# Seven products of layer 1 in another order, one weight sum by VectorE; the last chunk block by block, the last norm by VectorE alone

## The chip, the core and the metric

The kernel runs on one core of a Trainium2 chip, as one launch. The metric is the device time in microseconds, median of several runs. The engines of a core are TensorE (PE in the profile; its weight loads PEld), VectorE (DVE), ScalarE (ACT), GpSimd (POOL) and SyncE (SP), which here issues DMAs. Each engine works through its own queue in order.

## The reference, cut to what matters

Two layers of a backbone over 512 latent tokens of width 2048 (and 256 context tokens, which only layer 0 uses). The change is in layer 1:

```python
xm = x_lat * (1.0 + sc_l) + sh_l                       # 512 x 2048
u, v, z = jnp.split(xm @ w_in, 3, axis=-1)             # w_in 2048 x 6144
v = layer_norm(v, ln_g, ln_b)
s = jnp.einsum('hts,bnshc->bnthc', w_sp, vh) + b_sp    # per 128 tokens and head
y = u * s * jax.nn.silu(z)
x = layer_norm(alpha * x_lat + g_l * (y @ w_out), post_ln_g, post_ln_b)   # w_out 2048 x 2048
```

All of it is float32. A product is made of three matmuls: each operand is split into a high part (rounded to the type fp32r) and a low part, the rest; high x high, high x low and low x high are added up.

## The kernel before, in words

**Layer 1's input product** is done in six jobs of 1024 columns, n = 0 to 5: two for v (`first` = 2, those with a `place`), then z, u, z, u. Each job is a 2 by 2 block product done with seven half-size products in place of eight. A product p has four steps, j = 0 to 3; one step is 12 matmuls of 128x512 (L1226 to L1228). The list `self.steps` in the class `Quarters` sets the order of TensorE's work. In it products 1 and 2 of jobs 0 and 1 stand first (as a block, while the context of layer 1's input is still being made), then for each job the groups of L1149.

A product's weight operand is a quarter of the weights (`wq`, 512 KB per step) or a sum of quarters. How each operand comes about:
- A raw load by SP (`raw`, tile `qr`) goes to one of four raw buffers (`crw0` and three `wraw`), in turn.
- In jobs 0 and 1 sums are made by DMAs that POOL issues and that add into what lies in the tile (`add`, L1163). Product 7 adds two quarters in a raw tile. A pair tile per j (`t1`) is loaded and added to for product 5, added to again for 6 (after 5's operand is split), and again for 4 (after 6's).
- In jobs 2 to 5 VectorE makes the sums of products 1 and 7 (L1203 and L1197); the pair tile still gets its additions for 6 and 4 from POOL.

`split` (L104 to L106) makes each operand's high part on ScalarE (L105) and its low part on VectorE (L106). They go to seven unit buffers in turn. `prep` runs two steps ahead of TensorE's step (QAHEAD), the loads three more (LAHEAD).

**The evacuation** of a finished product (`run`, L1237 to L1270) adds and subtracts the products' results and hands blocks to a `sink`. `combine` (before L1117) makes the activations' sums for products 5, 7, 6 and 3 of all jobs and splits them.

**The output product** (`out_phase` L953, `form_b` L186) goes in four chunks of 512 columns. For each of 16 row blocks of the weights (a part; `weights`, `ahead`), it does 3 matmuls (L202 to L204) for each of four blocks of 128 tokens. In the last chunk this holds for the first 4 parts only. The other 12 (HOLD) are kept, and each token block takes them in one go. When a token block is done, VectorE evacuates it (L964, L965, L967), and the final norm follows (`norm1`, L1408): three quarters of the row by VectorE (L1418, L1419), one by POOL, ScalarE and POOL (L1413 to L1416). POOL also takes the power for the standard deviation (L246). Each quarter is stored by its own DMA.

Of the kernel before, what the change touches and what calls it, by code (L numbers as in the profile page):

```python
# [10 lines left out]
F32 = mybir.dt.float32  # L11
# [57 lines left out]
def tile_backbone(ctx: ExitStack, tc: tile.TileContext, io: dict, out: bass.AP):  # L69
# [74 lines left out]
    AHEAD, HOLD = 2, 12  # L144
# [12 lines left out]
    def ahead(p):  # L157
        while len(parts) < min(p + AHEAD + 1, 2 * upto[0]):
# [6 lines left out]
            held = q - (2 * len(stream) - 8)  # L165
            if held >= 0:
                hi = big.tile([P, 512], F32R, tag=f"xh{2 * held}", name=nm("wh"))
                lo = big.tile([P, 512], F32R, tag=f"xh{2 * held + 1}", name=nm("wl"))
            else:
                hi, lo = halves()  # L170
# [917 lines left out]
    def combine():  # L1088
# [21 lines left out]
        for g in range(4):  # L1110
            after(ve.tensor_tensor, comb[3, g], comb[6, g], comb[3, g], ALU.subtract)
            yield PACE
            after(comb_split, 3, g, (big, f"xh{2 * g}"), (big, f"xh{2 * g + 1}"))
            yield PACE
        free = [f"mr{n}" for n in (4, 5, 6, 7, 0, 1, 2)] + ["mx"]
        for g in range(4):
            after(comb_split, 6, g, (la, free[2 * g]), (la, free[2 * g + 1]))  # L1117
            yield PACE
# [20 lines left out]
    class Quarters:  # L1139
# [5 lines left out]
        def __init__(self, jobs, first):  # L1145
            self.jobs, self.first = jobs, first
            self.steps = [(n, p_, j) for p_ in (1, 2) for n in range(first) for j in range(4)]
            for n in range(len(jobs)):
                for group in ((5, 7), (3,), (6,), (4,)) if n < first else ((1, 5, 7), (2, 3), (6,), (4,)):  # L1149
                    self.steps += [(n, p_, j) for j in range(4) for p_ in group]  # L1150
            self.rtags, self.utags = ["crw0"] + ["wraw"] * 3, ["araw"] * 3 + ["whl"] * 4
            self.n_r = self.n_u = 0
            self.loaded, self.made, self.t1 = [], [], {}
# [10 lines left out]

        def load(self, n, p_, j):
            first = n < self.first
            if p_ == 5 and first:
                self.t1[j] = pair_tile(j)
                dma.dma_start(self.t1[j], io["wq"][self.jobs[n][0], j, 1])
                self.add(self.t1[j], n, j, 0)  # L1170
                rs = []
            elif p_ == 7 and first:
                rs = [self.raw(n, j, 1)]
                self.add(rs[0], n, j, 3)
            elif p_ == 1 and not first:
                rs = [self.raw(n, j, 1), self.raw(n, j, 0)]
            else:
                rs = [self.raw(n, j, {1: 0, 7: 3, 2: 2, 3: 3}[p_])] if p_ in (1, 7, 2, 3) else []
            self.loaded.append(rs)
# [6 lines left out]
        def prep(self, upto):  # L1186
            while len(self.made) < min(upto, len(self.steps)):
# [5 lines left out]
                if p_ in (5, 6, 4):  # L1193
                    x_ = self.t1[j]
                elif p_ == 7 and n >= self.first:
                    x_ = self.b12[j]
                    ve.tensor_tensor(x_, x_, rs[0], ALU.add)  # L1197
                else:
                    x_ = rs[-1]
                    if p_ == 1 and n >= self.first:  # L1200
                        self.b12 = getattr(self, "b12", {})
                        self.b12[j], self.t1[j] = rs[0], pair_tile(j)
                        ve.tensor_tensor(self.t1[j], x_, rs[0], ALU.add)  # L1203
# [3 lines left out]
                if p_ in (5, 6):  # L1207
                    self.add(self.t1[j], n, j, 3 if p_ == 5 else 2)

        def run(self):  # L1210
            bank, w_, q57 = {}, {}, {}
            for i, (n, p_, j) in enumerate(self.steps):
# [17 lines left out]
                if p_ == 4 and j > 1:  # L1230
                    sink(*c22[j - 2])
                if j < 3:
                    continue
                neg = lambda x_: lambda o: ve.scalar_tensor_tensor(o, x_[0], -1.0, x_[1], ALU.mult, ALU.subtract)
# [7 lines left out]
                elif p_ == 5:  # L1242
                    q57[n] = [la.tile([P, 512], F32, tag="t2", name=nm("qc"), bufs=4) for _ in range(2)]
                    for t in range(2):
                        sc.copy(q57[n][t], pts[t])
                elif p_ == 7:
                    for t in range(2):
# [289 lines left out]
```

## Time and profile before

| | |
|---|---|
| median of 3 runs | 1743.78 us (1741.64 to 1746.02) |
| the profiled run | 1744.94 us |
| its span | 1743.1 us |
| mean granted clock of TensorE | 0.994 |
| PE busy | 98% of the span |
| DVE, ACT, POOL busy | 68%, 39%, 5% |
| DMA | 366.62 MB, mean 210 GB/s |

Durations in the text are from the profiled run; its span is 1.84 us shorter than its time. Times within the span count from its start. PE's busy share is an average: where TensorE waits is seen in windows, not here.

### The profile page before, as it was taken

To read this page: it belongs to the slowest core of one execution; us is meant where nothing else is said; L and a number is where in the kernel's file an instruction comes from. 1 tells how busy PE (TensorE), PEld (TensorE's weight loads), DVE (VectorE), ACT (ScalarE), POOL (GpSimd) and SP (SyncE) were. 2 spreads that over 40 slices of the span, in tenths; PEclk is the share of its full clock that TensorE was granted. 3 is DMA by queue.
4 is the path that set the end of the run, shared out by engine and by line. 5 is a ranking of instruction groups with operands and counts; after the bars stand their busy time and mean duration, and the time that the engine had idled before them with its cause. 6 is when DMAs were issued, how large, how long until landed. Compare 5 with 4: busy or idle time off the path is not lost.

```text
span 1743.1 us, 22763 instructions
## 1 busy us (share of the span) xinstructions
PE 1709.7 (98%) x8260; PEld 1398.9 (80%) x8260; DVE 1193.1 (68%) x2113; ACT 686.3 (39%) x1190; POOL 94.4 (5%) x129
## 2 busy tenths in 40 slices
PE   9999999999999999999999999989999999999995
PEld 5777788888888888888888888868887888788884
DVE  5875486556798886867644478857775767665557
ACT  4222232323544454445432257533544354432221
POOL 0000000000000000000000001220100100000004
PEclk9999999999999999999999999999999999999998
DMA  9986277879678575663483568996757576665442
GB/s 344 374 318 226 85 245 239 285 261 324 222 266 282 197 247 169 219 199 110 131 256 121 145 232 269 238 237 161 238 140 225 138 231 139 197 167 162 131 140 101
DMA packets 143295, 366.62 MB, mean 210 GB/s; under 512 B 13522, under 2 KB 29866, under 8 KB 142670
## 3 DMA queue, kind: packets, MB, share of 16 engines
q1 hardware_dynamic: 126574, 322.69, 54.6%
q0 software_dynamic: 9216, 33.56, 10.7%
q10 hardware_dynamic: 7392, 8.91, 1.4%
q8 instruction: 65, 1.06, 0.2%
q14 instruction: 48, 0.39, 0.1%
HBM read 340.42 MB, written 24.69 MB: 209 GB/s over the span
## 4 chain that ended last, share of the span: by engine, by line
PE 89%; DMA 5%; DVE 4%; issue 1%; ACT 0%; POOL 0%; POOLq 0%; ACTq 0%; DVEq 0%; SPq 0%
PE ps L202 10%; PE ps L204 10%; PE ps L203 10%; PE ps L1227 7%; PE ps L1228 7%; PE ps L1226 7%; PE ps L187 6%; PE ps L186 6%; PE ps L191 6%; PE ps L455 2%; PE ps L457 2%; PE ps L671 2%; PE ps L456 2%; DMA qr<-in_wq_dram 2%; DMA pair<-in_wq_dram 1%; PE ps L374 1%
## 5 line engine op out<-in xcount | busy, mean ns | idle before, releaser
L105 ACT CAST wh<-wr 128x512 fp32r<-128x512 f32 x344 | 211.7, 621 | 467.8 <-PE ps L204 284.2
L106 DVE TENSOR_TENSOR wh<-wr,wh 128x512 fp32r<-128x512 f32 x336 | 230.0, 687 | 208.1 <-ACT wh L105 206.3
L204 PE MATMUL ps<-wh,yl 128*128 128x512 f32 x512 | 199.5, 390 | 0.0
L202 PE MATMUL ps<-wh,yh 128*128 128x512 f32 x512 | 193.6, 391 | 0.0
L203 PE MATMUL ps<-wh,yh 128*128 128x512 f32 x480 | 187.2, 390 | 0.0
L186 PE MATMUL ps<-xh,wh 128*128 128x512 f32 x448 | 175.5, 392 | 0.0
L187 PE MATMUL ps<-xl,wh 128*128 128x512 f32 x448 | 174.8, 390 | 0.0
L191 PE MATMUL ps<-xh,wh 128*128 128x512 f32 x448 | 174.6, 390 | 0.0
L272 DVE SCALAR_TENSOR_TENSOR adw<-adw,crow 128x1024 f32<-128x1024 f32 x128 | 155.8, 1217 | 3.3 <-DMA adw<-in_adat_dram 3.2
L1227 PE MATMUL ps<-wh,ch 128*128 128x512 f32 x384 | 150.6, 395 | 4.0 <-DVE wh L106 4.0
L1228 PE MATMUL ps<-wh,ch 128*128 128x512 f32 x384 | 150.0, 394 | 0.0
L1226 PE MATMUL ps<-wh,ch 128*128 128x512 f32 x384 | 145.3, 400 | 3.6 <-ACT wh L105 3.6
L105 ACT CAST wh<-qr 128x1024 fp32r<-128x1024 f32 x96 | 100.9, 1057 | 117.7 <-DMA qr<-in_wq_dram 49.2
L106 DVE TENSOR_TENSOR wh<-qr,wh 128x1024 fp32r<-128x1024 f32 x96 | 116.6, 1220 | 34.4 <-PE ps L1227 11.7
L106 DVE TENSOR_TENSOR wh<-pair,wh 128x1024 fp32r<-128x1024 f32 x72 | 87.9, 1221 | 55.1 <-PE ps L1227 21.3
L105 ACT CAST wh<-pair 128x1024 fp32r<-128x1024 f32 x72 | 75.8, 1053 | 107.0 <-PE ps L1228 41.3
L1227 PE MATMUL ps<-wh,xn 128*128 128x512 f32 x288 | 113.1, 393 | 1.4 <-DVE wh L106 1.3
L1228 PE MATMUL ps<-wh,xn 128*128 128x512 f32 x288 | 112.4, 390 | 0.0
L202 PEld LDWEIGHTS ps<-wh,yh 128*128 128x128 f32 x512 | 96.0, 188 | 19.9
L204 PEld LDWEIGHTS ps<-wh,yl 128*128 128x128 f32 x512 | 96.1, 188 | 19.7
L1226 PE MATMUL ps<-wh,xn 128*128 128x512 f32 x288 | 106.8, 395 | 2.3 <-ACT wh L105 2.3
L203 PEld LDWEIGHTS ps<-wh,yh 128*128 128x128 f32 x480 | 90.1, 188 | 18.5
(314 smaller groups left out, 3278.9 us busy)
## 6 DMA issues: line engine op xcount, KB each, us to landing
adw<-in_adat_dram SPq DMA_DIRECT2D x128, 512.0 KB, 5.1
qr<-in_wq_dram SPq DMA_DIRECT2D x112, 512.0 KB, 4.8
wr<-in_wie_dram SPq DMA_DIRECT2D x60, 512.0 KB, 3.3
pair<-in_wq_dram POOLq DMA_DIRECT2D x56, 512.0 KB, 7.2
aw<-in_a_dram SPq DMA_DIRECT2D x52, 512.0 KB, 5.9
wr<-in_woe_dram SPq DMA_DIRECT2D x40, 512.0 KB, 4.4
wr<-in_woo_dram SPq DMA_DIRECT2D x32, 512.0 KB, 3.9
wr<-in_wv_dram SPq DMA_DIRECT2D x16, 512.0 KB, 5.0
```

The costliest lines, as they stand in the source:

```text
L105: sc.copy(hi, src)
L106: return ve.tensor_tensor(lo, src, f32(hi), ALU.subtract)
L186: te.matmul(pt[:, :n], a, xh_, start=first, stop=False)
L187: te.matmul(pt[:, :n], a, xl_, start=False, stop=False)
L191: te.matmul(pt[:, :n], b, xh_, start=False, stop=last)
L202: te.matmul(pts[t], a, wh, start=n == 0, stop=False)
L203: te.matmul(pts[t], a, wl, start=False, stop=False)
L204: te.matmul(pts[t], b, wh, start=False, stop=n == KB - 1)
L272: ve.scalar_tensor_tensor(ts[n], ts[n], 0.5, crow[k], ALU.mult, ALU.mult, accum_out=part[:, f % 4, k:k + 1])
L1226: te.matmul(pts[t], a, wh[:, s], start=first, stop=False, **more)
L1227: te.matmul(pts[t], a, wl[:, s], start=False, stop=False, **more)
L1228: te.matmul(pts[t], b, wh[:, s], start=False, stop=end, **more)
```

## The change

- *Order of the steps.* Job 0: 5 and 7 by turns, then 6, 3, 4 (before: 3, 6, 4). Job 1: 7, 5, 6, 3, 4, each with its four steps together (before: 5 and 7 by turns, 3, 6, 4). Jobs 2 to 5: 1, 5, 7 by turns; 2 and 3 by turns for j = 0, 1; 2 for j = 2, 3; 6; 3 for j = 2, 3; 4 (before: 2 and 3 by turns for all j, 6, 4). The evacuations follow the new order, and `combine` splits the operand of 6 ahead of that of 3, with other tile names.
- *One weight sum.* In job 1 product 7's two quarters are both loaded by SP, and VectorE adds them (new L1210), where POOL's DMA added the second. The pair tiles of job 1 are loaded right behind the split of job 0's product 4.
- *The last chunk of the output product.* HOLD is 16, so all weight parts are kept, and token block 0 takes all 16 before block 1 begins. The look-ahead grows by up to four parts near the end, and four more parts lie in buffers of the input product.
- *The last norm.* All four quarters are normalised by VectorE.

```diff
@@ -141,7 +141,8 @@
         stream += b_raws(io["woo"], c)
     raws, parts, used, newest, older = [], [], [0], [None], [None]
 
-    AHEAD, HOLD = 2, 12
+
+    AHEAD, HOLD = 2, 16
...
     def ahead(p):
-        while len(parts) < min(p + AHEAD + 1, 2 * upto[0]):
+        last = p - (2 * len(stream) - HOLD)
+        more = min(max(last + 9, 0), 4) if last < 0 else 4
+        while len(parts) < min(p + AHEAD + more + 1, 2 * upto[0]):
             q = len(parts)
...
-            held = q - (2 * len(stream) - 8)
-            if held >= 0:
-                hi = big.tile([P, 512], F32R, tag=f"xh{2 * held}", name=nm("wh"))
-                lo = big.tile([P, 512], F32R, tag=f"xh{2 * held + 1}", name=nm("wl"))
+            held = q - (2 * len(stream) - HOLD)
+            if held >= 8:
+                hi = big.tile([P, 512], F32R, tag=f"xh{2 * held - 16}", name=nm("wh"))
+                lo = big.tile([P, 512], F32R, tag=f"xh{2 * held - 15}", name=nm("wl"))
+            elif 0 <= held < 4:
+                tag = ("araw", "araw", "crw0", "crw1")[held]
+                t = wp.tile([P, 1024], F32R, tag=tag, name=nm("wh"), bufs=3 if held < 2 else 1)
+                hi, lo = t[:, 0:512], t[:, 512:1024]
             else:
                 hi, lo = halves()
...
         for g in range(4):
             after(ve.tensor_tensor, comb[3, g], comb[6, g], comb[3, g], ALU.subtract)
             yield PACE
-            after(comb_split, 3, g, (big, f"xh{2 * g}"), (big, f"xh{2 * g + 1}"))
+            after(comb_split, 6, g, (big, f"xh{2 * g}"), (big, f"xh{2 * g + 1}"))
             yield PACE
-        free = [f"mr{n}" for n in (4, 5, 6, 7, 0, 1, 2)] + ["mx"]
+        free = [f"mr{n}" for n in (0, 1, 2, 3, 4, 5, 6)] + ["mx"]
         for g in range(4):
-            after(comb_split, 6, g, (la, free[2 * g]), (la, free[2 * g + 1]))
+            after(comb_split, 3, g, (la, free[2 * g]), (la, free[2 * g + 1]))
...
@@ -1146,11 +1153,11 @@
             self.jobs, self.first = jobs, first
             self.steps = [(n, p_, j) for p_ in (1, 2) for n in range(first) for j in range(4)]
             for n in range(len(jobs)):
-                for group in ((5, 7), (3,), (6,), (4,)) if n < first else ((1, 5, 7), (2, 3), (6,), (4,)):
-                    self.steps += [(n, p_, j) for j in range(4) for p_ in group]
+                for group, js in ((((5, 7), range(4)), ((6,), range(4)), ((3,), range(4)), ((4,), range(4))), (((7,), range(4)), ((5,), range(4)), ((6,), range(4)), ((3,), range(4)), ((4,), range(4))))[n] if n < first else (((1, 5, 7), range(4)), ((2, 3), range(2)), ((2,), (2, 3)), ((6,), range(4)), ((3,), (2, 3)), ((4,), range(4))):
+                    self.steps += [(n, p_, j) for j in js for p_ in group]
...
+        def load_t1(self, n, j):
+            self.t1[n, j] = pair_tile(j)
+            dma.dma_start(self.t1[n, j], io["wq"][self.jobs[n][0], j, 1])
+            self.add(self.t1[n, j], n, j, 0)
+
         def load(self, n, p_, j):
             first = n < self.first
-            if p_ == 5 and first:
-                self.t1[j] = pair_tile(j)
-                dma.dma_start(self.t1[j], io["wq"][self.jobs[n][0], j, 1])
-                self.add(self.t1[j], n, j, 0)
-                rs = []
-            elif p_ == 7 and first:
+            if first and p_ == 7 and n == 0:
                 rs = [self.raw(n, j, 1)]
                 self.add(rs[0], n, j, 3)
+            elif first and p_ == 7:
+                rs = [self.raw(n, j, 1), self.raw(n, j, 3)]
             elif p_ == 1 and not first:
                 rs = [self.raw(n, j, 1), self.raw(n, j, 0)]
             else:
                 rs = [self.raw(n, j, {1: 0, 7: 3, 2: 2, 3: 3}[p_])] if p_ in (1, 7, 2, 3) else []
+                if first and p_ == 5 and n == 0:
+                    self.load_t1(n, j)
...
                 while len(self.loaded) < min(i + 1 + LAHEAD, len(self.steps)):
                     self.load(*self.steps[len(self.loaded)])
                 rs = self.loaded[i]
-                if p_ in (5, 6, 4):
-                    x_ = self.t1[j]
-                elif p_ == 7 and n >= self.first:
-                    x_ = self.b12[j]
-                    ve.tensor_tensor(x_, x_, rs[0], ALU.add)
-                else:
-                    x_ = rs[-1]
-                    if p_ == 1 and n >= self.first:
-                        self.b12 = getattr(self, "b12", {})
-                        self.b12[j], self.t1[j] = rs[0], pair_tile(j)
-                        ve.tensor_tensor(self.t1[j], x_, rs[0], ALU.add)
+                if p_ == 1 and len(rs) == 2:
+                    self.b12[j], self.t1[n, j] = rs[0], pair_tile(j)
+                    ve.tensor_tensor(self.t1[n, j], rs[1], rs[0], ALU.add)
+                x_ = self.t1[n, j] if p_ in (5, 6, 4) else rs[-1]
+                if p_ == 7 and (len(rs) == 2 or n >= self.first):
+                    x_ = rs[0] if n < self.first else self.b12[j]
+                    ve.tensor_tensor(x_, x_, rs[-1], ALU.add)
                 self.made.append((self.unit(), self.unit()))
                 newest[0] = split(x_, *self.made[-1])
 
                 if p_ in (5, 6):
-                    self.add(self.t1[j], n, j, 3 if p_ == 5 else 2)
+                    self.add(x_, n, j, 3 if p_ == 5 else 2)
+                elif p_ == 4 and n + 1 < self.first:
+                    self.load_t1(n + 1, j)
...
                 fl.pe(12 * 0.216)
-                if p_ == 4 and j > 1:
-                    sink(*c22[j - 2])
+                if p_ == 4 and j < 2:
+                    sink(2 + j, 1, None, neg((q57[n][j], w_[n][j])))
...
-                elif p_ == 5:
-                    q57[n] = [la.tile([P, 512], F32, tag="t2", name=nm("qc"), bufs=4) for _ in range(2)]
-                    for t in range(2):
-                        sc.copy(q57[n][t], pts[t])
-                elif p_ == 7:
-                    for t in range(2):
-                        ve.tensor_tensor(q57[n][t], pts[t], q57[n][t], ALU.add)
+                elif p_ in (5, 7):
+                    if n not in q57:
+                        q57[n] = [la.tile([P, 512], F32, tag="t2", name=nm("qc"), bufs=4) for _ in range(2)]
+                        for t in range(2):
+                            sc.copy(q57[n][t], pts[t])
+                    else:
+                        for t in range(2):
+                            ve.tensor_tensor(q57[n][t], pts[t], q57[n][t], ALU.add)
                 elif p_ == 6:
                     for t in range(2):
                         ve.tensor_tensor(w_[n][t], w_[n][t], pts[t], ALU.subtract)
-                    if not place:
-                        for t in range(2):
-                            sink(t, 1, None, neg((bank[n, 5][t], w_[n][t])))
-                    c22 = [(2 + t, 1, None, neg((q57[n][t], w_[n][t]))) for t in range(2)]
+                elif p_ == 3 and not place:
+                    for t in range(2):
+                        sink(t, 1, None, neg((pts[t], w_[n][t])))
...
@@ -1406,17 +1418,10 @@
             y_out(n + 3)
 
     def norm1(t, z, m2, r_):
-        nb_ = la.tile([P, 1], F32, tag="nb", name=nm("nb"), bufs=2)
         for c in range(4):
             s = slice(c * 512, (c + 1) * 512)
-            if c == 0:
-                gp.tensor_scalar(nb_, m2[:, 0:1], -1.0, r_[:, 0:1], ALU.mult, ALU.mult)
-                sc.activation(z[:, s], z[:, s], AF.Identity, bias=nb_[:, 0:1], scale=r_[:, 0:1])
-                gp.tensor_tensor(z[:, s], z[:, s], lnr[0, c], ALU.mult)
-                gp.tensor_tensor(z[:, s], z[:, s], lnr[1, c], ALU.add)
-            else:
-                ve.scalar_tensor_tensor(z[:, s], z[:, s], m2[:, 0:1], lnr[0, c], ALU.subtract, ALU.mult)
-                ve.scalar_tensor_tensor(z[:, s], z[:, s], r_[:, 0:1], lnr[1, c], ALU.mult, ALU.add)
+            ve.scalar_tensor_tensor(z[:, s], z[:, s], m2[:, 0:1], lnr[0, c], ALU.subtract, ALU.mult)
+            ve.scalar_tensor_tensor(z[:, s], z[:, s], r_[:, 0:1], lnr[1, c], ALU.mult, ALU.add)
             dma.dma_start(out[t * P:(t + 1) * P, s], z[:, s])
```

On POOL, at the turn from job 0 to job 1 (`pair_1702` to `pair_1728` are job 0's four pair tiles, `qr_` raw tiles of job 1's product 7, `pair_1790` and those behind it job 1's pair tiles). Before:

```order
L1163 DMA pair_1728_9989<-in_wq_dram 128x1024
L1163 DMA qr_1793_10315<-in_wq_dram 128x1024
L1163 DMA qr_1799_10353<-in_wq_dram 128x1024
L1163 DMA qr_1807_10406<-in_wq_dram 128x1024
L1163 DMA pair_1702_9845<-in_wq_dram 128x1024
L1163 DMA qr_1817_10449<-in_wq_dram 128x1024
L1163 DMA pair_1710_9893<-in_wq_dram 128x1024
L1163 DMA pair_1716_9935<-in_wq_dram 128x1024
L1163 DMA pair_1728_9989<-in_wq_dram 128x1024
L1163 DMA pair_1790_10294<-in_wq_dram 128x1024
```

The same place of POOL's queue after the change:

```order
L1170 DMA pair_1728_9989<-in_wq_dram 128x1024
L1170 DMA pair_1702_9845<-in_wq_dram 128x1024
L1170 DMA pair_1710_9893<-in_wq_dram 128x1024
L1170 DMA pair_1716_9935<-in_wq_dram 128x1024
L1170 DMA pair_1728_9989<-in_wq_dram 128x1024
L1170 DMA pair_1790_10284<-in_wq_dram 128x1024
```

The four additions into raw tiles, three of which stood ahead of job 0's addition into `pair_1702` and one between it and `pair_1710`, are gone.

On VectorE, the same turn after the change (`wh_` are low parts from L106; `pair_1702` to `pair_1728` are product 4 of job 0, `qr_1791` and `qr_1796` product 7 of job 1; L1223 and L1301 belong to the evacuation of job 0):

```order
L1210 TENSOR_TENSOR qr_1791_10299<-qr_1791_10299,qr_1792_10301 128x1024
L1223 SCALAR_TENSOR_TENSOR v_1807_10371<-qc_1753_10118,v_1650_9611 128x512
L106 TENSOR_TENSOR wh_1787_10265<-qr_1771_10196,wh_1786_10264 128x1024
L1301 BN_STATS vst_1371_8072<-v_1801_10345 128x6
L106 TENSOR_TENSOR wh_1789_10281<-pair_1702_9845,wh_1788_10280 128x1024
L1301 BN_STATS vst_1372_8073<-v_1807_10371 128x6
L1210 TENSOR_TENSOR qr_1796_10322<-qr_1796_10322,qr_1797_10324 128x1024
L106 TENSOR_TENSOR wh_1794_10304<-pair_1710_9893,wh_1793_10303 128x1024
L106 TENSOR_TENSOR wh_1799_10327<-pair_1716_9935,wh_1798_10326 128x1024
L106 TENSOR_TENSOR wh_1805_10353<-pair_1728_9989,wh_1804_10352 128x1024
L106 TENSOR_TENSOR wh_1811_10380<-qr_1791_10299,wh_1810_10379 128x1024
L106 TENSOR_TENSOR wh_1813_10397<-qr_1796_10322,wh_1812_10396 128x1024
```

Before, no sum of raw tiles stood there. Now the first stands ahead of the splits of job 0's last product 3 and first product 4, the second ahead of the other three of product 4. The third and fourth (not shown) stand each ahead of its own split, behind these.

On VectorE at the end of the program, the last token block (`z_2300` before, `z_2304` after). Before:

```order
L964 TENSOR_TENSOR z_2300_13212<-ps_2439_14186,pair_2333_13384 128x512
L1419 SCALAR_TENSOR_TENSOR z_2299_13211<-z_2299_13211,rst_2482_14490,lnr_2368_13575 128x512
L965 SCALAR_TENSOR_TENSOR z_2300_13212<-xres_2458_14303,z_2300_13212 128x512
L967 BN_STATS st_2304_13216<-z_2300_13212 128x6
L1014 BN_AGGR m2_2484_14546<-st_2304_13216 128x2
```

And after:

```order
L1424 SCALAR_TENSOR_TENSOR z_2303_13219<-z_2303_13219,rst_2484_14480,lnr_2372_13583 128x512
L971 TENSOR_TENSOR z_2304_13220<-ps_2449_14210,pair_2337_13392 128x512
L972 SCALAR_TENSOR_TENSOR z_2304_13220<-xres_2471_14293,z_2304_13220 128x512
L974 BN_STATS st_2308_13224<-z_2304_13220 128x6
L1021 BN_AGGR m2_2485_14545<-st_2308_13224 128x2
```

The norm of the block before (`z_2299`, `z_2303`) no longer reaches into the last block's evacuation.

## Rows read from the trace of the kernel before

**Rows 1.** The page: the chain that ended last, by engine.
```profile
PE 89%; DMA 5%; DVE 4%; issue 1%; ACT 0%; POOL 0%; POOLq 0%; ACTq 0%; DVEq 0%; SPq 0%
```

**Rows 2.** Windows: stretch, length, busy us (xinstructions) by engine, granted clock, DMA share, GB/s.
```profile
1080.00:1120.00 40.00, 40.00 (x178) 33.15 (x177) 35.78 (x48) 28.54 (x43) 7.86 (x9) 1.00 0.92 231
1120.00:1160.00 40.00, 36.07 (x152) 27.70 (x151) 21.74 (x26) 12.51 (x14) 10.13 (x12) 1.00 1.02 229
1160.00:1200.00 40.00, 38.55 (x167) 31.22 (x168) 27.20 (x28) 17.98 (x19) 6.46 (x8) 1.00 0.94 226
...
1320.00:1360.00 40.00, 37.33 (x157) 30.01 (x156) 24.94 (x25) 19.84 (x23) 3.48 (x4) 0.96 0.68 202
...
1480.00:1520.00 40.00, 38.20 (x169) 31.03 (x168) 23.81 (x23) 18.61 (x23) 1.72 (x2) 0.96 0.71 213
```

**Rows 3.** The chain of waits, 1118 to 1150: start us, us, what.
```profile
1120.79 1.15 DVE wh L106
...
1122.00 6.26 DMA qr<-in_wq_dram
...
1130.31 0.83 POOL qr L1163
...
1133.59 8.74 DMA pair<-in_wq_dram
...
1142.41 1.05 ACT wh L105
```

**Rows 4.** POOL's timeline at the turn from job 0 to job 1.
```profile
1118.74 0.87 POOL L1163 DMA_DIRECT2D qr<-in_wq_dram  x1 [10.44 <-ACT ch L105]
```

**Rows 5.** Waits from 1116 to 1170: us in total, times, longest.
```profile
ACT wh L105 <- DMA pair<-in_wq_dram: 22.7, 7, 5.6
...
PE ps L1226 <- ACT wh L105: 3.0, 4, 1.3
```

**Rows 6.** The chain of waits, 1294 to 1330.
```profile
1297.60 4.97 DMA qr<-in_wq_dram
...
1304.90 1.23 DVE qr L1197
...
1316.57 8.26 DMA qr<-in_wq_dram
```

**Rows 7.** TensorE's timeline: the last matmul.
```profile
1725.06 0.39 PE L204 MATMUL ps<-wh,yl 128*128 128x512 f32 x1
```

**Rows 8.** POOL's timeline at the end of the program.
```profile
1729.88 1.59 POOL L1416 TENSOR_TENSOR z<-z,lnr 128x512 f32<-128x512 f32 x1
...
1737.73 1.59 POOL L1416 TENSOR_TENSOR z<-z,lnr 128x512 f32<-128x512 f32 x1
```

**Rows 9.** The page: DMA queues and issues of the output weights.
```profile
q1 hardware_dynamic: 126574, 322.69, 54.6%
q0 software_dynamic: 9216, 33.56, 10.7%
...
wr<-in_woo_dram SPq DMA_DIRECT2D x32, 512.0 KB, 3.9
```

**Rows 10.** VectorE's timeline: token block 0 of the last chunk, then the last block.
```profile
1706.90 0.69 DVE L964 TENSOR_TENSOR z<-ps,pair 128x512 f32<-128x512 f32 x1 [3.39 <-PE ps L204]
1707.62 0.69 DVE L965 SCALAR_TENSOR_TENSOR z<-xres,z 128x512 f32<-128x512 f32 x1
...
1709.45 2.07 DVE L1418 SCALAR_TENSOR_TENSOR z<-z,m,lnr 128x512 f32<-128x512 f32 x3
1711.43 0.75 DVE L1419 SCALAR_TENSOR_TENSOR z<-z,rst,lnr 128x512 f32<-128x512 f32 x1
...
1730.27 1.75 DVE L965 SCALAR_TENSOR_TENSOR z<-xres,z 128x512 f32<-128x512 f32 x1
...
1735.13 3.07 DVE L1419 SCALAR_TENSOR_TENSOR z<-z,rst,lnr 128x512 f32<-128x512 f32 x3
```

**Rows 11.** VectorE's timeline, two neighbours in the last chunk.
```profile
1689.00 0.67 DVE L106 TENSOR_TENSOR wl<-wr,wh 128x512 fp32r<-128x512 f32 x1
1689.61 0.67 DVE L996 TENSOR_TENSOR xres<-xres,pair 128x512 f32<-128x512 f32 x1
```

More of the change, by code (lines that the diff above doesn't have):

```diff
@@ L1148, in __init__ @@
             for n in range(len(jobs)):
-                for group in ((5, 7), (3,), (6,), (4,)) if n < first else ((1, 5, 7), (2, 3), (6,), (4,)):
-                    self.steps += [(n, p_, j) for j in range(4) for p_ in group]
+                for group, js in ((((5, 7), range(4)), ((6,), range(4)), ((3,), range(4)), ((4,), range(4))), (((7,), range(4)), ((5,), range(4)), ((6,), range(4)), ((3,), range(4)), ((4,), range(4))))[n] if n < first else (((1, 5, 7), range(4)), ((2, 3), range(2)), ((2,), (2, 3)), ((6,), range(4)), ((3,), (2, 3)), ((4,), range(4))):
+                    self.steps += [(n, p_, j) for j in js for p_ in group]
             self.rtags, self.utags = ["crw0"] + ["wraw"] * 3, ["araw"] * 3 + ["whl"] * 4
             self.n_r = self.n_u = 0
-            self.loaded, self.made, self.t1 = [], [], {}
+            self.loaded, self.made, self.t1, self.b12 = [], [], {}, {}
         def raw(self, n, j, piece):
@@ L1207, in prep, with neg @@
                 if p_ in (5, 6):
-                    self.add(self.t1[j], n, j, 3 if p_ == 5 else 2)
+                    self.add(x_, n, j, 3 if p_ == 5 else 2)
+                elif p_ == 4 and n + 1 < self.first:
+                    self.load_t1(n + 1, j)
         def run(self):
             bank, w_, q57 = {}, {}, {}
+            def neg(x_):
+                return lambda o: ve.scalar_tensor_tensor(o, x_[0], -1.0, x_[1], ALU.mult, ALU.subtract)
             for i, (n, p_, j) in enumerate(self.steps):
@@ L1229, in run @@
                 fl.pe(12 * 0.216)
-                if p_ == 4 and j > 1:
-                    sink(*c22[j - 2])
+                if p_ == 4 and j < 2:
+                    sink(2 + j, 1, None, neg((q57[n][j], w_[n][j])))
                 if j < 3:
                     continue
-                neg = lambda x_: lambda o: ve.scalar_tensor_tensor(o, x_[0], -1.0, x_[1], ALU.mult, ALU.subtract)
                 if p_ == 1:
@@ L1304, in spatial @@
             dma.dma_start(wsp, io["wsp"][:, 2 * c:2 * c + 2, :])
-            g_ = la.tile([P, 512], F32, tag="mr3", name=nm("lg"))
+            g_ = la.tile([P, 512], F32, tag="mr7", name=nm("lg"))
             dma.dma_start(g_, io["sgug"][:, s].to_broadcast([P, 512]))
@@ L1312, in spatial @@
                 yield pace
-            b_ = la.tile([P, 512], F32, tag="mr3", name=nm("lb"))
+            b_ = la.tile([P, 512], F32, tag="mr7", name=nm("lb"))
             dma.dma_start(b_, io["sgub"][:, s].to_broadcast([P, 512]))
```

## Prediction

> **What bounds the kernel now.** The page comes first. TensorE is busy for 98% of the span and holds 89% of the chain that ended last; DMA holds 5% and VectorE 4% [rows 1]. The work of TensorE is the same in both kernels (the same products, the same 128x512 matmuls), so only two things can change the time: stretches in which TensorE stands, and what comes after its last matmul. I look for each in turn.
>
> The windows show the first. In an undisturbed 40 us TensorE starts 178 matmuls, so one takes 40/178 = 0.225 us. From 1120 to 1160 it started 152 and from 1160 to 1200 it started 167 [rows 2]: 26 + 11 = 37 matmuls too few, 37 x 0.225 = 8.3 us of standing. That is the end of job 0 and the start of job 1. The DMA share there is 1.02 and 0.94, so the queues are full as well. Two later windows, 1320 and 1480, lack 21 and 9 (6.8 us, a granted clock of 0.96 included).
>
> The chain of waits names what stood in the way in 1120 to 1145. It goes from VectorE's split at 1120.79 to a raw load (1122.00, 6.26 us), to a POOL DMA that adds into this raw tile (1130.31), and only from there to POOL's next DMA, which adds into a pair tile (1133.59, 8.74 us to land), whose split (1142.41) TensorE waits for [rows 3]. The reader is to see the jump from a raw tile (`qr`) to a pair tile. They are different sums: the first is job 1's sum for product 7, the second is job 0's sum for product 4. They meet only because POOL issues in order. POOL's own rows say the same: the add into `qr` at 1118.74 was waited for 10.44 us [rows 4], with the adds of job 0 behind it. In 1116 to 1170 ScalarE waited seven times, 22.7 us, for the landing of such pair sums, and TensorE's own stalls stand behind that wait [rows 5].
>
> The later windows have another cause. From 1295 to 1327 the chain is raw load (4.97), VectorE sum L1197 (1.23), raw load (8.26) and so on [rows 6]: four raw buffers in turn, no POOL.
>
> At the end the last matmul starts at 1725.06 and takes 0.39, to 1725.45 [rows 7]. The last arithmetic is POOL's L1416 at 1737.73, for 1.59, to 1739.32 [rows 8]; the span ends 3.8 later at 1743.1, which is the last store. So 13.9 us lie between the last product and the last value.
>
> **The change part by part.** *Order of the steps and the sum of product 7, jobs 0 and 1.* Four accumulating DMAs leave POOL's queue, so job 0's adds for product 4 no longer stand behind job 1's sums. Also, a pair tile is needed again 8 steps after its last split, where it was 4 (6 to 4, and 4 of job 0 to 5 of job 1). A step is 12 matmuls, 12 x 0.225 = 2.7 us, so the add has 21.6 us where it had 10.8. It needs POOL's 0.9 to issue and up to 8.74 to land [rows 3]; the split takes another 1.05 on ScalarE and about 1.2 on VectorE. That is 11.9, above 10.8 and far under 21.6. By this all 8.3 us go. The DMA work falls too. Estimated from the queues, an accumulating transfer of 0.524 MB costs 10.7% of 1743.1 us over 33.56/0.524 = 64, 2.9 us of all sixteen engines, and a plain one 54.6% over 322.69/0.524 = 616, 1.5 us [rows 9]. Four times 1.4 is 5.5 us less in a stretch whose share is 1.02.
>
> What is added: four VectorE sums of 1.23 each [rows 6], and four plain loads in SP's queue. VectorE is busy for 21.7 of 40 us in the first window [rows 2], so the 4.9 us themselves are hidden. The order puts the first two sums ahead of splits that product 3 and product 4 of job 0 need, and VectorE is in order, so a late load would hold these splits. Bounds: nothing if all eight loads are there; 21 us if each sum holds VectorE for a whole turn of the raw buffers (worked out under the slower rival). I take 1.5 us, near the lower end: the buffers of the first four loads come free by the splits of product 3, and four steps of product 4 (10.9 us), which take no raw buffer, lie between; the third and fourth sum have less room. Gain: 8.3 - 1.5 = 6.8.
>
> *Order in jobs 2 to 5.* The chain of [rows 6] starts in products 1, 5 and 7 of a job, whose order, buffers and VectorE sums stay. What moves is behind them (2, 3, 6, 4). I take 0, with 3 us either way: better if the raw loads of 3, spread apart, let the next job's come earlier; worse if they land in the same pile. The tile renamings and the swap of splits 6 and 3 in the combinations move work beside TensorE by one place each; nothing there is waited for in job 0, 0.
>
> *Last norm by VectorE alone.* Block 0 shows VectorE's part undisturbed: from L964 at 1706.90 to L1418 at 1709.45 are 2.55 us, one L1418 follows another after 0.66, and the single L1419 took 0.75 [rows 10]. After the change the last block is 1725.5 + 2.55 + 4 x 0.66 + 3 x 0.66 + 0.75 = 1733.4, and POOL's power (1 us) is done beside the first four. Now it is 1739.3. The store follows as before: 5.9 us gained. Two things leave together here. The chain POOL nb, ScalarE, POOL, POOL goes. So does the wait of the last block's start on the norm of block 2, because a block lasts 48 x 0.225 = 10.8 us and its norm 7.9.
>
> In [rows 10] VectorE's L965 took 0.69 at 1707.62 with POOL idle and 1.75 at 1730.27 while POOL ran L1416 (1729.88 [rows 8]), and three L1419 took 3.07 at 1735.13, where three L1418 took 2.07. The Trainium skill (SBUF — State Buffer, Who interferes with whom) says that a VectorE instruction with two inputs in SBUF contends with a GpSimd instruction that reads SBUF, and that the loser is blocked for the other's whole instruction. By that rule the excess goes with POOL's instructions, and the gain is 5.9; if these lengths were the instructions' own, it would be 1.06 + 1.0 less, 3.8.
>
> *Last chunk by single blocks.* TensorE now wants all 16 weight parts in block 0, where 4 parts by 4 blocks came first. By the order, VectorE has 28 instructions of 128x512 (evacuation of the chunk before, splits, residual) from 1.9 us before the chunk to the end of them. They start 0.61 apart [rows 11], 17 us, so the last ends 15.2 us into the chunk. The split of part 15 is about the 19th, at 9.9 us. TensorE reaches it after 15 parts of 3 matmuls (10.1) and 13 matmuls of block 1 that stand earlier (2.9), at 12.3 to 13. For part 7 it is 3.5 against 5, for part 14 7.5 against 11.6. The loads land in 3.9 [rows 9] and are asked for earlier than now, by four parts. So I take 0; the cover is 1.5 to 4 us. If it is gone, the price is 15.2 - 12.3 = 3 us where the splits come last of the 28, and twice that where a late load holds them as well.
>
> **The sum.** Profiled run 1744.94 - 6.8 - 5.9 = 1732.2. That run lies 1.16 above the median of 1743.78, so on the median's scale 1731.1; I say 1731.5.
>
> **The rivals.** *The standing only moves.* The DMA engines are full from 1120 to 1200, and the stall comes back wherever sums are late. For it: the share of 1.02. Against it: POOL's queue, not bandwidth, is in the chain, and 5.5 us of DMA work leave. Then only the tail is gained: 1743.8 - 5.9 = 1737.9, or 1736 with a third of the rest.
>
> *Jobs 2 to 5 gain as well.* Their standing (6.8 us in the two windows) shrinks by most: 1731.5 - 5 = 1726.5. For it: the second half of each job is reordered. Against it: the chain in [rows 6] starts before that half.
>
> *The last chunk starves.* The splits come late by the 3 to 6 us above: 1734.5 to 1737.5. For it: VectorE has no pause in these 17 us. Against it: the order puts the splits first.
>
> *Slower: the sums hold VectorE.* L1210 stands at the head of VectorE's queue until two raw loads have landed, with four raw buffers. A buffer's turn is load 8.26, sum 1.23, two halves of a split 1.05 and 1.2: 11.7 us, and two steps last 5.4. Each sum then holds the queue for some 5 to 6 us, behind it the splits that TensorE is next to want: three or four times, 16 to 21 us in place of 8.3. Less the tail, 1743.8 + 8 to 13 - 5.9 = 1746 to 1751. It is slower than before from 14.2 us of standing (8.3 + 5.9), and visibly so from 19. For it: the 8.26 of [rows 6] is just such a load before just such a sum. Against it: it came where three products of a job each wanted raws; here four steps without any lie ahead. The Trainium skill (DMA: Bandwidth & Descriptors, Queues, rings and completion order) adds to its side that a DMA engine takes turns between its queues packet by packet, so that a plain load beside POOL's adds gets a part of the engine only. The landing of 6.26 beside an add [rows 3] against 3.9 in the last chunk [rows 9] agrees.
>
> **How the numbers follow.** Forecast 0.58 (1727.5 to 1735 by its unknown costs), standing only moves 0.13, jobs 2 to 5 gain too 0.08, last chunk starves 0.08, slower 0.08, something else 0.05. A measurement here can tell 0.3%, 5.2 us: faster is under 1738.5, slower over 1749.0. The forecast and the third case are faster, most of the second and the fourth are as well, by little; half of the slower case passes 1749. Faster 0.79, same 0.14, slower 0.07. From 1726 to 1740 lie the forecast, the second, the fourth and half of the third: 0.8.
>
> **What would show it.** In the profile after, 1120 to 1200 should start about 350 matmuls (before 152 + 167), POOL's add into a pair tile should no longer be waited for by a raw tile's, and no long wait of VectorE's L1210 for a raw load should stand there. The windows of jobs 2 to 5 should read as now. The last L1424 should end about 8 us after the last matmul, with no VectorE instruction of over 0.8 us, and TensorE should start a matmul every 0.23 us through block 0 of the last chunk. A wait of TensorE on splits there, or on ScalarE at 1130 to 1170, would make the forecast wrong.

## The result, and the profile after

The changed kernel takes 1732.74 us (median of 4, 1732.04 to 1734.89) against 1744.12 before. The ratio is 0.9938, 95% interval 0.992 to 0.9955. Measured again in five rounds beside its parts it was 0.995 (0.9936 to 0.9964). So it is faster by 9 to 11 us, where 12.7 were summed up and 1731.5 us forecast; the time lies in the range. All ratios here are of executions in the chip's fast state, which leaves out one of no_jobs25 that took 3471.68 us.

The sum came out, its terms did not. To see that, the profiled runs of before and after are cut into sections by counting TensorE's matmuls (12 to a step). Times in us. "Job 2 to the end of products" runs from the first matmul of job 2 to the start of the program's last one, the tail from there to the end of the span. What lies ahead of job 0 took 1.2 us longer in after; it is the same program in both:

| | before | after | forecast of the difference | difference |
|---|---|---|---|---|
| job 0 (20 steps) | 59.3 | 54.6 | -6.8 | -4.8 |
| job 1 (20 steps) | 57.6 | 60.9 | with job 0 | +3.3 |
| job 2 to the end of products | 513.8 | 506.9 | 0 | -6.9 |
| tail | 18.0 | 12.2 | -5.9 | -5.8 |

The page of after: the chain by engine, then the DMA queues. DMA lost one point of the chain, VectorE two [rows 1]; 2.1 MB, four transfers, went from the queue of POOL's DMAs to SP's [rows 9].

```profile
PE 93%; DMA 4%; DVE 2%; issue 1%; ACT 0%; DVEq 0%; ACTq 0%
...
q1 hardware_dynamic: 127150, 324.78, 55.4%
q0 software_dynamic: 8640, 31.46, 10.2%
```

Windows of after, columns as in [rows 2]:

```profile
1120.00:1160.00 40.00, 37.54 (x163) 30.04 (x162) 31.66 (x38) 15.14 (x16) 5.24 (x6) 1.00 0.95 255
1160.00:1200.00 40.00, 38.85 (x164) 31.57 (x163) 26.69 (x27) 15.60 (x16) 6.98 (x8) 0.96 0.88 212
```

There 327 matmuls start, where 319 did and about 350 were expected. The granted clock, 1.00 in both windows before, is 0.96 in the second. (That is this pair: four of the five other profiles of the old order in jobs 0 and 1 have 0.96 in one of the two windows as well.) The chain of waits of after, 1118 to 1178, without TensorE's pieces, then TensorE's timeline:

```profile
1144.75 1.24 DVE wh L106
1146.00 9.46 DMA qr<-in_wq_dram
1155.49 1.23 DVE qr L1210
```

```profile
1157.92 0.73 PE L1239 MATMUL ps<-wh,ch 128*128 128x512 f32 x2 [2.16 <-ACT wh L105]
```

No POOL stands in this chain any more, as forecast. In its place stand a split that frees raw buffers, a load of 9.46 us into them, and VectorE's new sum (the third of four). TensorE waits 2.16 us for ScalarE's half of the split behind it. From 1160.0 to 1163.3 its matmuls then start 0.43 apart, as at the lower of its two levels (1.2 GHz), and at 1173.2 it stands 1.15 us more. ScalarE's and VectorE's waits in 1140 to 1185 say the same:

```profile
ACT wh L105 <- DVE qr L1210: 12.5, 2, 10.9
...
DVE qr L1210 <- DMA qr<-in_wq_dram: 3.2, 1, 3.2
```

The end of the program, VectorE's timeline of after:

```profile
1718.39 0.69 DVE L971 TENSOR_TENSOR z<-ps,pair 128x512 f32<-128x512 f32 x1 [0.67 <-PE ps L211]
1719.11 0.69 DVE L972 SCALAR_TENSOR_TENSOR z<-xres,z 128x512 f32<-128x512 f32 x1
...
1720.93 2.73 DVE L1423 SCALAR_TENSOR_TENSOR z<-z,m,lnr 128x512 f32<-128x512 f32 x4
1723.58 2.73 DVE L1424 SCALAR_TENSOR_TENSOR z<-z,rst,lnr 128x512 f32<-128x512 f32 x4
```

The last matmul starts at 1717.96 and ends at 1718.35. The last value stands at 1726.31, 7.96 us later (13.9 before, 8.0 forecast). VectorE waited for TensorE, not the other way, and no instruction is longer than 0.8 us, where L965 had 1.75 beside POOL [rows 10].

### The profile page after: what moved, and what is told of

Read it like the earlier page. It is cut to its first block, busy times and chain, and to the rows that moved or that the text cites. A ratio compares the mean times of both kernels' runs of the same rounds, so it can differ in the third digit from the quotient of the medians.

```text
span 1730.2 us, 22749 instructions
## 1 busy us (share of the span) xinstructions
PE 1708.0 (99%) x8260; PEld 1399.3 (81%) x8260; DVE 1197.7 (69%) x2125; ACT 681.0 (39%) x1186; POOL 74.4 (4%) x113
## 4 chain that ended last, share of the span: by engine, by line
PE 93%; DMA 4%; DVE 2%; issue 1%; ACT 0%; DVEq 0%; ACTq 0%
PE ps L211 11%; PE ps L209 11%; PE ps L210 11%; PE ps L1240 7%; PE ps L1241 7%; PE ps L1239 7%; PE ps L193 6%; PE ps L194 6%; PE ps L198 6%; DMA qr<-in_wq_dram 3%; PE ps L462 2%; PE ps L464 2%; PE ps L463 2%; PE ps L678 2%; PE ps L381 1%; PE ps L686 1%
## 5 line engine op out<-in xcount | busy, mean ns | idle before, releaser
L106 DVE TENSOR_TENSOR wh<-wr,wh 128x512 fp32r<-128x512 f32 x336 | 229.9, 687 | 205.3 <-ACT wh L105 203.8
L105 ACT CAST wh<-qr 128x1024 fp32r<-128x1024 f32 x96 | 101.1, 1058 | 137.1 <-DMA qr<-in_wq_dram 56.7
L106 DVE TENSOR_TENSOR wh<-qr,wh 128x1024 fp32r<-128x1024 f32 x96 | 116.6, 1220 | 28.8 <-PE ps L1240 15.0
L106 DVE TENSOR_TENSOR wh<-pair,wh 128x1024 fp32r<-128x1024 f32 x72 | 87.6, 1221 | 40.8 <-PE ps L1240 20.3
L1240 PE MATMUL ps<-wh,xn 128*128 128x512 f32 x288 | 112.6, 391 | 0.0
```

The costliest lines, as they stand in the source:

```text
L105: sc.copy(hi, src)
L106: return ve.tensor_tensor(lo, src, f32(hi), ALU.subtract)
L1240: te.matmul(pts[t], a, wl[:, s], start=False, stop=False, **more)
```

## The experiments

All were timed in five rounds beside the kernel before. Four sets shared their rounds: norm_only, tail_only, jobs01_only and jobs25_only; after_again, tail_and_jobs25, sum_by_pool and sum_mixed; no_jobs25, five_raws and five_raws_mixed; chunk_only. Across sets only the ratios can be compared. Sections as above, from one profile each, in us:

| run | ratio (95%) | job 0 | job 1 | job 2 to end of products | tail |
|---|---|---|---|---|---|
| norm_only | 1.0001 (0.9991 to 1.0011) | 60.7 | 56.6 | 507.5 | 18.1 |
| tail_only | 0.9974 (0.9963 to 0.9985) | 61.4 | 55.2 | 508.9 | 12.9 |
| chunk_only | 0.9967 (0.9952 to 0.9983) | 61.1 | 56.3 | 508.4 | 12.9 |
| jobs01_only | 0.9995 (0.9986 to 1.0005) | 54.8 | 61.3 | 510.2 | 17.8 |
| jobs25_only | 0.9994 (0.9985 to 1.0003) | 61.4 | 56.7 | 509.2 | 18.0 |
| after_again | 0.995 (0.9936 to 0.9964) | 54.6 | 60.5 | 509.8 | 12.2 |
| tail_and_jobs25 | 0.9961 (0.9948 to 0.9975) | 59.5 | 56.4 | 508.9 | 12.4 |
| no_jobs25 | 0.9951 (0.9938 to 0.9964) | 54.6 | 58.7 | 513.0 | 12.2 |
| sum_by_pool | 0.9936 (0.992 to 0.9952) | 54.6 | 57.2 | 509.2 | 12.4 |
| sum_mixed | 0.9936 (0.9923 to 0.9949) | 54.6 | 58.0 | 509.3 | 12.8 |
| five_raws | 0.997 (0.9958 to 0.9983) | 54.7 | 63.6 | 506.7 | 12.3 |
| five_raws_mixed | 0.9924 (0.9912 to 0.9937) | 55.5 | 59.0 | 503.7 | 12.2 |

**norm_only.** Before, with only the last norm changed:

```diff
-            if c == 0:
...
-                gp.tensor_tensor(z[:, s], z[:, s], lnr[1, c], ALU.add)
-            else:
+            ve.scalar_tensor_tensor(z[:, s], z[:, s], m2[:, 0:1], lnr[0, c], ALU.subtract, ALU.mult)
+            ve.scalar_tensor_tensor(z[:, s], z[:, s], r_[:, 0:1], lnr[1, c], ALU.mult, ALU.add)
```

> The kernel before with the last norm by VectorE alone, nothing else changed. My theory (the tail is a chain of evacuation and norm behind the last matmul): the last value comes about 8 us after the last matmul where it came 13.9 after, so 1744.1 - 5.8 = 1738.3 us (1737 to 1740), since a block of 36 matmuls, 8.2 us, is still just longer than its norm of 7.9. Rival (VectorE needs the longer blocks of the new last chunk to keep up): the norm of a block spills into the next block's evacuation, up to 3 us of the gain are lost, 1740 to 1742.

Nothing was gained: 1.0001, tail 18.1. The rival holds, and more strongly than it was put. VectorE's timeline:

```profile
1712.33 2.73 DVE L1411 SCALAR_TENSOR_TENSOR z<-z,m,lnr 128x512 f32<-128x512 f32 x4
1714.98 0.69 DVE L964 TENSOR_TENSOR z<-ps,pair 128x512 f32<-128x512 f32 x1
1715.58 2.73 DVE L1412 SCALAR_TENSOR_TENSOR z<-z,rst,lnr 128x512 f32<-128x512 f32 x4
...
1720.52 0.69 DVE L964 TENSOR_TENSOR z<-ps,pair 128x512 f32<-128x512 f32 x1 [0.88 <-PE ps L204]
...
1721.92 2.73 DVE L1411 SCALAR_TENSOR_TENSOR z<-z,m,lnr 128x512 f32<-128x512 f32 x4
```

When the last product is there (1720.52), VectorE has still to do the whole norm of the block before (from 1721.92), and the last one after it. The expectation had taken 36 matmuls, 8.2 us, between two blocks' ends. In the order the four blocks of the last chunk end at matmul 110, 136, 162 and 192 of 192: matmuls of later blocks are slipped in ahead. Between the ends are 26 to 30 matmuls, 5.9 to 6.8 us, and a norm takes VectorE 7.8.

**tail_only and chunk_only.** The first is norm_only with the new last chunk. The second is before with the new last chunk alone:

```diff
-    AHEAD, HOLD = 2, 12
+    AHEAD, HOLD = 2, 16
...
+            elif 0 <= held < 4:
+                tag = ("araw", "araw", "crw0", "crw1")[held]
```

> The kernel before with the last norm by VectorE alone and the last chunk block by block. My theory: the single blocks bring nothing to the tail and cost about 1 us inside the chunk, as the traces of before and after put it (last matmul 8.2 us earlier at the chunk product's start, 7.1 at its end): 1744.1 - 5.8 + 1 = 1739.3 us, the same as with the norm alone or up to 1 more. Rival (the block order is what frees VectorE): 1 to 3 us under the run with the norm alone.

> The kernel before with the last chunk block by block alone; the last norm still uses POOL and ScalarE for a quarter. With the norm alone nothing was gained, with both 4.5 us. Theory (what cost the time was the wait of the last block's evacuation on the norms of the blocks before it, since those blocks ended 26 matmuls, 5.9 us, apart and a norm takes 7.8; POOL's chain is the smaller part): with 48 matmuls between the ends the last block starts at once, and by the rows of before its chain is 2.55 for evacuation and sums, then POOL 1.0 and 0.9, ScalarE 0.8, POOL 1.5 and 1.6, so the last value comes 8.8 us after the last matmul where it came 13.9: 5.1 us gained, ratio 0.997, the last matmul to the end 12.9 us. Rival (the chunk and the norm each need the other): half or less of that, ratio 0.9985 or more, 15.5 us or more from the last matmul to the end.

tail_only has 0.9974: the rival, 4.7 us under norm_only where it said 1 to 3. chunk_only has 0.9967 and a tail of 12.9, just as worked out. TensorE's last row, VectorE's first and last of the last block and POOL's last in chunk_only:

```profile
1720.06 0.39 PE L211 MATMUL ps<-wh,yl 128*128 128x512 f32 x1
```

```profile
1720.48 0.69 DVE L971 TENSOR_TENSOR z<-ps,pair 128x512 f32<-128x512 f32 x1 [1.11 <-PE ps L211]
...
1725.01 3.07 DVE L1426 SCALAR_TENSOR_TENSOR z<-z,rst,lnr 128x512 f32<-128x512 f32 x3
```

```profile
1727.62 1.59 POOL L1423 TENSOR_TENSOR z<-z,lnr 128x512 f32<-128x512 f32 x1
```

VectorE was waiting when the product came, and POOL's chain ends 8.8 us behind the last matmul. So of the 5.9 us between 13.9 and 8.0 the single blocks bring 5.1. The norm brings nothing alone and 0.8 on top; by timing that rest can't be seen (0.9967 without it, 0.9974 with it).

**jobs01_only and jobs25_only.** Before with the change in jobs 0 and 1 alone, and in jobs 2 to 5 alone:

```diff
-                for group in ((5, 7), (3,), (6,), (4,)) if n < first else ((1, 5, 7), (2, 3), (6,), (4,)):
+                for group, js in (((5, 7), range(4)), ((3,), range(4)), ((6,), range(4)), ((4,), range(4))) if n < first else (((1, 5, 7), range(4)), ((2, 3), range(2)), ((2,), (2, 3)), ((6,), range(4)), ((3,), (2, 3)), ((4,), range(4))):
...
```

(This is jobs25_only's, without its evacuations, which follow the order; jobs01_only has the changed list for n < 2 and the old one else.)

> The kernel before with the change in jobs 0 and 1 alone (order, VectorE's sum for product 7, early loads of the pair tiles, splits of the combinations); jobs 2 to 5, last chunk and norm as before. Theory from the two traces: a new standing at job 1's product 7 (one turn of the raw buffers, about 4 us) eats most of what the POOL queue gives back, so 1.5 us are gained: 1742.5 (1741 to 1744). Rival (the prediction's step: the standing of 8.3 us falls to 1.5): 1737.3 (1736 to 1739); then the 4 us that the trace after shows in job 1 are a chance of that one run.

> The kernel before with the new order of jobs 2 to 5 alone. Theory from the two traces (the steps from the start of job 2 to the start of the output product took 7.9 us less): 1744.1 - 7.9 = 1736.2 (1735 to 1738). Rival (the prediction's step: the chain starts in products 1, 5 and 7, whose order stays, so nothing): 1744 (1742.5 to 1745.5), and the 7.9 us are run to run or follow from what jobs 0 and 1 left.

jobs01_only has 0.9995, which can't be told from no gain, with the trace's numbers again: job 0 in 54.8, job 1 in 61.3. That is the first theory. jobs25_only has 0.9994, the rival: the 6.9 us that the first two traces differ by in jobs 2 to 5 are not the order's. Five profiles of the old jobs 2 to 5 with a changed kernel's other parts lie between 507.5 and 513.0; the profile of before, 513.8, was above all of them. Over all profiles the section means 510.3 with the old order (six) and 508.0 with the new (eight, 503.7 to 509.8), so a gain of 1 to 2 us is not excluded.

**after_again, tail_and_jobs25, no_jobs25.** The whole change again, the whole without its part in jobs 0 and 1, and the whole without its part in jobs 2 to 5 (the diffs above, the other way).

> The changed kernel itself, to be measured in as many rounds as its parts. Theory that the parts add up: last chunk with norm -4.6 us, jobs 0 and 1 -0.9, jobs 2 to 5 -1.0, together -6.5, ratio 0.9963. Rival (the parts help one another, so that the standing of jobs 2 to 5 goes only with both orders): the ratio stays at 0.994, 4 us more than the sum. In the profile, the 40 steps of jobs 0 and 1 should last 115.5 us again (before: 116.6 to 118.2), with a VectorE sum L1210 waiting 3 us or more for a raw load.

> The changed kernel with the change in jobs 0 and 1 undone: new last chunk and norm, new order of jobs 2 to 5, old order and POOL's sums in jobs 0 and 1. Theory that parts add up: -4.6 - 1.0 = -5.6 us, ratio 0.9968, 1 us over the whole change at most. Rival (jobs 0 and 1 carry the rest of the gain): 3 us or more slower than the whole change, ratio 0.9974 as with the tail alone.

> The changed kernel with the order of jobs 2 to 5 undone (as before), all else as changed. It prices that order by taking it away. Theory from ten traces (job 2's start to the last matmul took 507.5 to 513.8 us in the old order, mean 510.1, and 506.9 to 509.8 in the new, mean 508.9): 1 us slower than the whole change, ratio to before 0.9955, and the 7.9 us between the first two traces are run to run. Rival (they are the order's): 5 us or more slower than the whole change, ratio 0.998.

after_again repeats the trace: 115.1 us for jobs 0 and 1, the third sum waiting 2.83 us for its load. Without the order of jobs 2 to 5 the ratio is 0.9951, with it (in other rounds) 0.995: that order is worth nothing that these rounds can tell. Without the part in jobs 0 and 1 it is 0.9961, 2 us over the whole in the same rounds, with intervals that overlap. The parts alone add up to 0.9963 (-4.5, -0.9 and -1.0 us), which is the upper end of the whole's interval in five rounds. That the parts help one another by 4 us is not shown; 1 to 2 us stay open.

**sum_by_pool and sum_mixed.** The whole change; job 1's sums of product 7 all by POOL, or those of j = 1 and 2:

```diff
-            if first and p_ == 7 and n == 0:
+            if first and p_ == 7:
```

```diff
-            if first and p_ == 7 and n == 0:
+            if first and p_ == 7 and (n == 0 or j in (1, 2)):
```

> The changed kernel with product 7's sum of job 1 made by POOL's accumulating DMA again, as before; order and early loads of the pair tiles stay as changed. It tells the order from the sum. Theory (the new standing in job 1 is one turn of the raw buffers, since a VectorE sum needs two of four): with one raw tile per sum all four are loaded during the four steps of product 4, the 9.5 us load ahead of a sum is gone, and jobs 0 and 1 take 112 us or less (115.5 with VectorE's sum): 3 to 4 us faster than the whole change. Rival (the queues are full there, and 4 more accumulating DMAs cost 5.5 us of transfer): the pair tiles of job 1's product 5 come late instead, jobs 0 and 1 take 115 to 117 us, no faster.

> The changed kernel with product 7's sum of job 1 by VectorE for j = 0 and 3 and by POOL's accumulating DMA for j = 1 and 2, so that the first three sums together take just the four raw buffers. Theory of the raw buffers' turn: only the fourth sum's loads wait for a buffer, and they have one step more; jobs 0 and 1 take 111 to 113 us, 3 us faster than the whole change. Rival (full queues): 115 us as in the whole change.

Both have lower medians than the whole change in the same rounds (1732.4 and 1731.3 against 1734.7), though the intervals of the ratios overlap, and jobs 0 and 1 take 111.8 and 112.6 us against 115.1. sum_by_pool in the windows, and the two longest pieces of its chain there:

```profile
1120.00:1160.00 40.00, 40.00 (x178) 33.00 (x177) 32.02 (x39) 15.93 (x17) 9.35 (x11) 1.00 0.98 242
1160.00:1200.00 40.00, 38.40 (x166) 30.47 (x165) 24.05 (x24) 16.47 (x17) 6.96 (x8) 1.00 0.95 241
```

```profile
1144.24 13.80 DMA pair<-in_wq_dram
...
1161.32 11.82 DMA pair<-in_wq_dram
```

TensorE does not stand at all from 1120 to 1160, and its clock stays. What is left (job 1 is 2.6 us longer than job 0) is the rival's: pair tiles, of product 5 and then 6, that land late in full queues. So the sum by VectorE cost job 1 the larger part of its loss (3.7 of 6.5 us in after), and the order with the early loads gave job 0 its gain. How much the sum costs varies. In the four profiles that have all four of VectorE's sums in four buffers the third sum waits 2.1 to 4.4 us for its load, and job 1 takes 58.7 to 61.3; the 58.7 is no_jobs25, where TensorE stood 0.99 us behind that sum and its clock did not fall. The four POOL DMAs that the change removed were not what held the pair tiles; their place ahead of them was.

**five_raws and five_raws_mixed.** The whole change with a fifth raw buffer in jobs 0 and 1; in the second with the sum of j = 1 by POOL as well:

```diff
...
-            tag = self.rtags[self.n_r % len(self.rtags)]
+            tags = self.rtags + ["crw1"] if n < self.first else self.rtags
+            tag = tags[self.n_r % len(tags)]
...
```

> The whole change, with a fifth raw buffer in jobs 0 and 1 (the 4 KB that later hold the evacuations' intermediate, free until job 2). VectorE still makes all four sums of product 7 in job 1. Theory of the raw buffers' turn: one of the third sum's two loads starts a turn earlier, the other still waits for a buffer of the first sum, so the load of 9 us ahead of L1210 stays and jobs 0 and 1 take 114 to 115.5 us, as with four buffers. If it were the count alone (each more buffer buys time) they would take 113 or less.

> The whole change with the fifth raw buffer and product 7's sum of j = 1 in job 1 by POOL's accumulating DMA: 2 + 1 + 2 raw tiles, so the first three sums of job 1 together take just the five buffers and only one accumulating DMA comes back. Theory of the raw buffers' turn: as with the mixed sums in four buffers or 1 us better, jobs 0 and 1 in 111 to 112.5 us, 3 to 4 us faster than the whole change, ratio to before 0.993. Rival (full queues decide): 113 us or more, no faster than the mixed sums.

five_raws missed both expected times: jobs 0 and 1 take 118.3 us, job 1 63.6 of them, and the ratio is 0.997. The last two of VectorE's four sums, then the chain ahead of the last:

```profile
1144.28 1.23 DVE L1211 TENSOR_TENSOR qr<-qr,qr 128x1024 f32<-128x1024 f32 x1 [1.63 <-DMA qr<-in_wq_dram]
...
1159.16 1.23 DVE L1211 TENSOR_TENSOR qr<-qr,qr 128x1024 f32<-128x1024 f32 x1 [6.14 <-DMA qr<-in_wq_dram]
```

```profile
1146.64 1.15 DVE wh L106
...
1147.80 11.34 DMA qr<-in_wq_dram
...
1159.16 1.24 DVE qr L1211
```

In VectorE's order of this program the sum at 1144.28 is that of j = 3, and the last is that of j = 2. With five buffers in turn, the second tile of j = 2 takes the buffer in which the sum of j = 0 lies. So its load starts when that sum is split (at 1147.8) and lands in 11.34 us, and TensorE stands 6.47 us for j = 2. That is the mechanism of the first theory: one load of the third sum comes earlier, the other still waits a turn. Only its size was off, by 2.8 us or more. five_raws_mixed is the fastest of all, 1729.86 us and 0.9924 (0.9912 to 0.9937). Its jobs 0 and 1 take 114.4 us in the profile, though, more than the 111 to 112.5 expected and than sum_mixed: that is the rival's figure, and VectorE's last sum there waits 4.43 us for a load of 10.35. Its jobs 2 to 5 are the shortest seen (503.7). So in this profile its lead over sum_mixed (intervals overlap) does not come from jobs 0 and 1, where the buffer was added; where it comes from is open.

## Why the prediction was right

The time was right partly by luck. Of the two large terms the tail (5.9) held. The larger, jobs 0 and 1 (6.8), fell short by 5 to 6 us. With that error alone the time would have been about 1737, above the forecast's own range (1727.5 to 1735) and near the rival by which the standing only moves (1736 to 1738). It came out at 1732.74 because the whole gained more than its measured parts, which no run explains. In its first rounds the whole gained 11.4 us by the medians, and 8.7 by the ratio of the later ones, against 12.3 forecast.

- *The tail, -5.9.* Measured -5.8 in the trace and 4.5 (0.9974) by timing. The rows were read rightly, down to the last value 8.0 us behind the last matmul. The gain was put under the wrong edit: all 5.9 stood under the norm and 0 under the chunk, and norm_only, chunk_only and tail_only turn that round. The working named both causes (POOL's chain, and the wait on block 2's norm) and did not price them apart; the first was 0.8, the second 5.1.
- *Where two VectorE inputs and POOL meet.* L972 took 0.69 with POOL idle. In chunk_only, which keeps POOL's part, three L1426 beside it took 3.07 again, and without POOL four L1424 took 2.73, 0.66 apart. That agrees with the Trainium skill (SBUF — State Buffer, Who interferes with whom), by which a VectorE instruction with two inputs in SBUF contends with a GpSimd instruction that reads SBUF.
- *The last chunk does not starve.* In after, all matmuls from 1674 to 1718 start no more than 0.24 us apart; the cover of 1.5 to 4 us was enough.
- *Jobs 0 and 1, -6.8.* This step failed. Its first half, that POOL's queue was the cause, held: job 0 takes 54.6 us, and 20 steps of 2.72 are 54.4; it shortened by 4.8 in the pair of traces and by 5.0 to 6.9 against the other traces of the old order. The second half, "I take 1.5 us" for the sums, was too low: job 1 became 3.3 longer, and the two jobs together still take 6.7 us more than 40 steps (108.8), where 1.5 were forecast and 8.1 stood before. TensorE's wait for ScalarE at 1157.92 is the sign that the prediction itself had named against this step. The reason given, that four steps without raws lie ahead, covers the first two sums only. The raws of these two fill all four buffers through those steps, so the third sum's loads start when the first is split, and land in 9.46. It is the mechanism of the slower rival, for one turn instead of three or four. In after the clock fell behind it as well, which the working had not priced; but it also fell at this turn in four of the six profiles of the old order. Net -1.4 in the pair of traces, about -2 by the mean of all (six with the old order, four with the new and all of VectorE's sums), -0.9 by timing of the part alone.
- *Jobs 2 to 5, 0 within 3.* Right within its 3 us by timing (0.9994 alone; 0.9951 with it undone, 0.995 with it). The pair of traces says -6.9, and would have misled without the others.
- *The sum.* The terms measured apart, -4.5, -0.9 and -1.0, make -6.4; the whole was -8.7 (-6.3 to -11.2) in the same manner and -10.8 in its first rounds. The sum forecast was -12.7: too much by 5.9 in jobs 0 and 1 and by 1.4 in the tail, too little by 1.0 in jobs 2 to 5. The 2 to 4 us that the whole has over its parts are not explained. -6.4 lies outside the interval of the first rounds (-7.8 to -14.0) and just inside that of the later ones, and each part's own interval is 1.6 to 1.9 us either way. The means of the sections would close the gap (about -2, -2 and -5.8), but single profiles of jobs 2 to 5 spread over 6 us.

## What to carry to other kernels

When two edits meet in one place, price each alone as well as both: here a shorter norm was worth nothing while blocks ended closer together (5.9 us) than a norm lasts (7.8), and the spacing has to be counted in the order of the instructions, not in the loops. A sum made of two loaded tiles takes two buffers through the whole stretch ahead of it; count which tiles lie in the buffers when the load should start, not only how long it has. Where profiles of the same code differ by 6 us in one section, as here, a difference between two profiles is not yet an effect: count the same section in several.

## What was not expected of the hardware

The fall of TensorE's clock did not go by the length of a stand. In before TensorE stood 0.95, 1.30, 0.76 and 0.52 us within 12 us, towards the end of job 0, and its granted clock stayed at 1.00. In tail_only it stood 2.39 us at 1139.4 and 1.89 us at 1156.9, and the clock stayed at 1.00 too. In tail_and_jobs25 it stood 0.91, 0.83 and 0.77 us, and from 1145.5 its matmuls started 0.43 apart instead of 0.227. In after it stood once for 2.16 us and 0.22 soon after, and the matmuls from 1160.0 to 1163.3 started 0.43 apart, which cost another 1.6 us. In five_raws, with a single stand of 6.47 us, the granted clock was 0.92 in 1160 to 1200:

```profile
1160.00:1200.00 40.00, 38.41 (x159) 31.28 (x160) 24.71 (x27) 17.92 (x19) 6.98 (x8) 0.92 0.87 200
```

A 512 KB load by SP landed in 4.7 us in the median of all raw loads of after. Around 1150 single ones took 9.5 (after), 11.3 (five_raws) and 13.8 us (a pair tile in sum_by_pool), with a DMA share of 0.91 to 0.98 in 1120 to 1160.
